# A hybrid decoder layer on one core: gate chunks beside the attention output projection, two plain blocks at the head of the second FFN, and the softmax combination's transfers on GpSimd's queue

## The chip, the cores and the metric

The kernel runs on one core of one Trainium2 chip. The metric is the time of one execution on the device, in microseconds (us), as the median of several runs. The engines are named as in the profile: PE is TensorE (the matmuls), PEld its weight loads, DVE is VectorE, ACT is ScalarE, POOL is GpSimd, SP is SyncE. SP computes nothing in this kernel and only issues DMAs; its issues are rows of "SPq".

## What is computed

One layer for 1024 prompt positions and 8 x 4 sample positions, 1056 rows of width 1024, in float32:

```
h  = LN1(alpha*x + 0.5*SwiGLU_a(x))                 # FFN-a, width 2816
z  = h @ w_in + b_in                                # q, k, v of 12 heads; u, v of the gMLP; gates gA, gB
A  = dilated sliding-window attention, 3 head groups (dilation 1, 4, 16), 4 heads each;
     head slot j of the 3 groups combined by their softmax denominators
B  = u * (tril(W_s) LN(v) + b)                      # gMLP, chunks of 128
h  = LN2(alpha*h + (sigmoid(gA)*(A@w_oa) + sigmoid(gB)*(B@w_ob)) @ w_out)
y  = LN3(alpha*h + 0.5*SwiGLU_b(h))                 # FFN-b
```

The updated key and value windows are outputs too; most of their bytes are copied from memory to memory (`ws<-st` in the profile).

## The kernel before, in words

**Layout.** Activations lie transposed, features on the 128 partitions and positions along the row. The 1056 positions are four chunks of 264 (`C`, `NC`). Every float32 operand is split into a high part (a cast on ACT, line 238) and a low part (a subtraction on DVE, line 239), and a product is three matmuls (`mm3`, line 227 for all of them). A product with a full 1024-row weight block is 24 matmuls for a chunk (`dense8`: a gate, a half of a plain FFN block, a block of w_out), one with w_ob 12, one with w_oa 6.

**Stages in order of time.** FFN-a (0 to about 650 us) and FFN-b (from about 1483) each have 22 blocks of 128 hidden features. Most blocks go through a Strassen-like scheme (`hidden`, seven products for all four chunks together, 168 matmuls); block 0 is computed plainly, chunk by chunk (`hidden8`, 48 matmuls a chunk), because a plain chunk can start as soon as its own layer norm is ready. In FFN-b the four chunks come out of LN2 one after the other. LN2 and LN3 are `norm`: column sums of squares on PE, a reciprocal root (`rsqrt`: a square root on ACT, line 630, and four small DVE operations), a broadcast by PE (line 597), scaling on DVE and ACT.

Between the FFNs comes `widen` (the input projection) and then `mix`, around which most of the change lies. In `mix` the PE's order is: ten "tail" gate blocks (6 block by block, then `LAST` = 4 together, chunk by chunk), then the w_ob products (`local(n)`, n = 0 to 5), then for each of the eight blocks n of w_oa: `product(wa, att, ...)` for the four chunks, each multiplied into the gate on DVE (line 1505), with `local(6)` and `local(7)` behind n = 0 and 1; then the sum of both branches (DVE, line 1583), its split, and w_out.

**What runs beside it.** Generators are advanced between these products (`tick`): `attend(i)` for six pairs of head slot and group (`bg`), the sample positions' attention (`slow`), the gMLP and the combination (`mid`). `attend` loads q, k and v of its pair from a scratch tensor (`fetch_qkv`, tiles `S<-zD`) and, at its start, those of the next pair; it ends with a transpose of the row maxima and sums (line 1225), which DVE copies out and a DMA writes to `mlD` (line 1229). After the third group of a head slot `combine(hp)` reads `mlD` back in another arrangement (lines 1247, 1249, 1253), computes the weights on DVE, writes them to `cD` (1276), reads them back spread over 64 partitions (1283) and scales and adds the three groups (1288 to 1291). The result, `att`, is split (`split_att`), and only then can w_oa start. All these transfers stand on SP's one queue, in order, between weights, gates and window copies.

**What sets the order.** Each engine executes its instructions in the order of the built program; a scheduler fixes it beforehand from priorities and a model of durations. Tiles come from pools of fixed size (37 large `S` slots, 8 weight buffers `W`, 2 raw buffers `R`, 3 + 5 PSUM banks `mm` and `ax`). An instruction that waits holds everything behind it on its engine.

Of the kernel before, what the change touches and what calls it, by code (L numbers as in the profile page):

```python
# [13 lines left out]
F32R = mybir.dt.float32r  # L14
AF = mybir.ActivationFunctionType
# [5 lines left out]
P = 128  # L21
# [43 lines left out]
WARM = 2  # L65
FENCED = (mybir.EngineType.DVE, mybir.EngineType.Activation, mybir.EngineType.SP)
# [4 lines left out]
LAST = 4  # L71
EARLY = 6
# [7 lines left out]
class Trunk:  # L80
# [131 lines left out]
    def unit(self, src, n=D, slot=False, ahead=URGENT):  # L212
        new = self.S if slot else self.W
        with self.tc.high_priority(offset=ahead):
            raw = self.R([P, D])
            hi, lo = new([P, D], F32R), new([P, D], F32R)
            dma = self.nc.sync.dma_start(raw[:, :n], src[:, :n])
            self.split(hi[:, :n], lo[:, :n], raw[:, :n])
        self.fence[mybir.EngineType.SP] = dma.ins
# [362 lines left out]
    def norm(self, c, i, mode, Y, s):  # L582
# [7 lines left out]
        r, t = self.X([P, 3], "rs"), self.X([P, 3], "rt")  # L590
        self.rsqrt(r, t, pv, EPL)
# [35 lines left out]

    def rsqrt(self, r, t, v, eps):
# [12 lines left out]
    def ffn(self, w13, w2p, w2, i, mode, resid):  # L641
        nc, preps = self.nc, {}
        last = FB + NG * (KB // 2) - 1
# [27 lines left out]
        else:  # L671
# [17 lines left out]
        def ready(f):  # L689
            for _ in preps.pop(f):  # L690
                pass
            if f < last:
                begin(f + 1)

        def between(f, bg, slow=0):
            if f + 1 in preps:
                next(preps[f + 1], None)
# [8 lines left out]
        for f in range(1, FB):  # L706
# [5 lines left out]
            def after():  # L712
# [4 lines left out]
            self.hidden(f, after)  # L717
# [400 lines left out]
    def attend(self, i):  # L1118
# [19 lines left out]
        self.fetch_qkv(i + 1)  # L1138
# [77 lines left out]
        for t in range(6):  # L1216
# [4 lines left out]
            if t < 4:  # L1221
                scores(t)
            yield from self.pause(SPREAD)
# [5 lines left out]
        nc.sync.dma_start(D_.rearrange("m h (i x) -> (m h i) x", x=P), mt)  # L1229
# [6 lines left out]
    def combine(self, hp):  # L1236
# [3 lines left out]
        for g in range(3):  # L1240
            x = raw[:, g]
            for m in range(2):
                for h in range(2):
                    src = self.mlD[hp, g, m, h]
                    o = x[8 * h : 8 * h + 8, m]
                    if g == 0:
                        nc.sync.dma_start(o, src.rearrange("(a x) -> a x", a=8))
                    elif g == 1:
                        nc.sync.dma_start(
                            o.rearrange("p (r b) -> p r b", r=4), src.rearrange("(r a b) -> a r b", r=4, a=8)  # L1250
                        )
                    else:
# [541 lines left out]
```

## Time and profile before

| | us |
|---|---|
| median of 3 runs | 2202.64 (2201.89 to 2203.19) |
| the profiled execution's own time | 2200.98 |
| its span, first to last instruction | 2199.2 |
| PE busy | 2133.2 |
| DVE busy | 1564.8 |
| ACT busy | 898.1 |
| POOL busy | 330.1 |

The profiled execution lies 1.66 us below the median. Of its own time, 1.8 us lie outside the span. PE is the engine with work nearly all the time, so time can be won where PE waits, or where it runs at a lower granted clock, and lost where PE gets more work or new waits. A window row of the profile gives busy time with the number of instructions in brackets for PE, PEld, DVE, ACT and POOL, then the granted PE clock, the busy share of the DMA engines and GB/s. A timeline row gives start, length, engine, line, operation, and in square brackets the idle time before it with what ended it.

### The profile page before, as it was taken

To read this page: it belongs to the slowest core of one execution; us is meant where nothing else is said; L and a number is where in the kernel's file an instruction comes from. 1 tells how busy PE (TensorE), PEld (TensorE's weight loads), DVE (VectorE), ACT (ScalarE), POOL (GpSimd) and SP (SyncE) were. 2 spreads that over 40 slices of the span, in tenths; PEclk is the share of its full clock that TensorE was granted. 3 is DMA by queue.
4 is the path that set the end of the run, shared out by engine and by line. 5 is a ranking of instruction groups with operands and counts; after the bars stand their busy time and mean duration, and the time that the engine had idled before them with its cause. 6 is when DMAs were issued, how large, how long until landed. Compare 5 with 4: busy or idle time off the path is not lost.

```text
span 2199.2 us, 43234 instructions
## 1 busy us (share of the span) xinstructions
PE 2133.2 (97%) x17281; PEld 2092.9 (95%) x17281; DVE 1564.8 (71%) x2718; ACT 898.1 (41%) x1690; POOL 330.1 (15%) x238
## 2 busy tenths in 40 slices
PE   9999999999998999999989998998999999999997
PEld 8999999999998999999879897998999999999997
DVE  8777776656788725887674648778676776657787
ACT  5444444421225634344465354246444444322224
POOL 0432332200010022232000000000432332100000
PEclk9999999999999999999989999999999999999999
DMA  4435545598873325666854547513445545596751
GB/s 157 146 134 177 179 161 177 193 367 324 330 279 136 135 102 188 215 215 221 313 165 152 172 156 245 187 51 126 165 158 178 171 161 185 186 384 264 295 192 79
DMA packets 170553, 429.82 MB, mean 195 GB/s; under 512 B 24864, under 2 KB 61456, under 8 KB 167664
## 3 DMA queue, kind: packets, MB, share of 16 engines
q1 hardware_dynamic: 169920, 426.53, 55.3%
q8 instruction: 135, 2.21, 0.4%
q10 hardware_dynamic: 432, 0.54, 0.1%
q14 instruction: 66, 0.54, 0.1%
HBM read 305.97 MB, written 167.22 MB: 215 GB/s over the span
## 4 chain that ended last, share of the span: by engine, by line
PE 81%; DMA 7%; DVE 7%; ACT 2%; issue 1%; POOL 1%; SPq 1%; ACTq 0%; DVEq 0%; POOLq 0%
PE ax L227 43%; PE mm L227 35%; DMA M<-kv 4%; DVE W L239 1%; PE ax L1164 1%; DMA zD<-M 1%; DMA S<-zD 1%; PE ax L1203 1%; DVE S L239 1%; PE ax L1187 1%; DMA R<-wz 0%; DVE X L1346 0%; DVE S L608 0%; DVE X L1361 0%; DVE M L1345 0%
## 5 line engine op out<-in xcount | busy, mean ns | idle before, releaser
L227 PE MATMUL ax<-S,W 128*128 128x264 f32 x5472 | 716.2, 284 | 0.8 <-ACT S L994 0.5
L227 PE MATMUL mm<-S,W 128*128 128x264 f32 x5040 | 677.4, 289 | 25.8 <-DVE S L1505 9.3
L227 PEld LDWEIGHTS ax<-S,W 128*128 128x128 f32 x5472 | 685.6, 188 | 3.3 <-ACT S L994 1.5
L227 PEld LDWEIGHTS mm<-S,W 128*128 128x128 f32 x5040 | 641.6, 191 | 43.1 <-issue 10.7
L227 PE MATMUL ax<-S,S 128*128 128x264 f32 x3288 | 483.7, 285 | 2.9 <-DVE S L1003 2.8
L227 PEld LDWEIGHTS ax<-S,S 128*128 128x128 f32 x3288 | 434.2, 188 | 4.1 <-DVE S L1003 4.1
L227 PE MATMUL mm<-S,S 128*128 128x264 f32 x2496 | 388.4, 286 | 9.0 <-ACT S L238 4.0
L227 PEld LDWEIGHTS mm<-S,S 128*128 128x128 f32 x2496 | 337.7, 189 | 11.5 <-ACT S L238 4.4
L238 ACT CAST W<-R 128x256 fp32r<-128x256 f32 (+2 forms) x172 | 127.6, 759 | 316.8 <-PE mm L227 118.2
L369 POOL TENSOR_TENSOR Q<-R 128x512 f32<-128x512 f32 x50 | 72.1, 1443 | 793.1 <-DMA R<-w13b 217.1
L239 DVE TENSOR_TENSOR W<-R,W 128x256 fp32r<-128x256 f32 (+2 forms) x172 | 152.6, 891 | 28.2 <-ACT W L238 24.0
L238 ACT CAST W<-Q 128x1024 fp32r<-128x1024 f32 (+1 forms) x79 | 77.9, 986 | 217.1 <-POOL Q L370 91.7
L780 DVE SCALAR_TENSOR_TENSOR S<-ax,S 128x264 f32<-128x264 f32 x240 | 99.9, 431 | 69.6 <-PE ax L227 68.5
L444 DVE TENSOR_TENSOR S<-ax,M 128x264 f32<-128x264 f32 x84 | 33.7, 433 | 150.6 <-PE ax L227 150.6
L106 POOL CAST S<-ones 128x1 fp32r<-128x1 f32 x32 | 18.3, 594 | 745.5 <-PE mm L227 663.8
L239 DVE TENSOR_TENSOR S<-Q,S 128x1024 fp32r<-128x1024 f32 (+1 forms) x79 | 111.8, 1415 | 3.5 <-ACT S L238 3.3
L239 DVE TENSOR_TENSOR W<-Q,W 128x1024 fp32r<-128x1024 f32 (+1 forms) x79 | 92.0, 1164 | 24.5 <-ACT W L238 24.5
L238 ACT CAST S<-Q 128x1024 fp32r<-128x1024 f32 (+1 forms) x79 | 77.8, 985 | 74.1 <-PE ax L227 55.0
L238 ACT CAST S<-R 128x512 fp32r<-128x512 f32 (+1 forms) x65 | 44.6, 686 | 116.5 <-DMA sumsA<-S 42.6
L239 DVE TENSOR_TENSOR S<-S,M 128x528 fp32r<-128x528 f32 x72 | 85.6, 1189 | 2.1 <-ACT M L238 0.2
L370 POOL TENSOR_TENSOR Q<-Q,R 128x512 f32<-128x512 f32 x50 | 83.6, 1673 | 2.7
L377 POOL TENSOR_TENSOR Q<-R,Q 128x512 f32<-128x512 f32 x50 | 82.7, 1653 | 1.2
(199 smaller groups left out, 2063.3 us busy)
## 6 DMA issues: line engine op xcount, KB each, us to landing
ws<-st SPq DMA_DIRECT2D x144, 256.0 KB
S<-sumsA SPq DMA_DIRECT2D x63, 528.0 KB
S<-sumsB SPq DMA_DIRECT2D x63, 528.0 KB
M<-kv SPq DMA_DIRECT2D x96, 256.0 KB
sumsA<-M SPq DMA_DIRECT2D x90, 264.0 KB
sumsB<-M SPq DMA_DIRECT2D x90, 264.0 KB
R<-w13b SPq DMA_DIRECT2D x44, 512.0 KB
S<-zD SPq DMA_DIRECT2D x42, 528.0 KB
```

What stands on the lines that cost most here:

```text
L106: self.nc.gpsimd.tensor_copy(t[:, 0, :1] if len(shape) == 3 else t[:, :1], self.ones[:, :1])
L227: mm = lambda a, b, s, e: nc.tensor.matmul(o, a[:, cc], b, start=s, stop=e, skip_group_check=True)
L238: a = self.nc.scalar.copy(hi, src)
L239: b = self.nc.vector.tensor_tensor(lo, src, hi.bitcast(F32), op=ALU.subtract)
L369: tt(s12[:, lo], cd[:, lo], cd[:, hi], op=ALU.add)
L370: tt(s12[:, hi], s12[:, lo], ab[:, lo], op=ALU.subtract)
L377: tt(s34[:, hi], ab[:, hi], s12[:, hi], op=ALU.subtract)
L444: go(one, 5, False, lambda x: tt(h[:, x, 1], one[x], p7[:, x], op=ALU.add))
L780: nc.vector.scalar_tensor_tensor(y(x, r, e), bank[x], HALF, y(x, r, e), op0=ALU.mult, op1=ALU.add)
L1164: nc.tensor.matmul(pS[h][:, r, :nk], q[e, i * P : (i + 1) * P], k[e, k0 : k0 + nk], start=True, stop=True)
L1187: nc.tensor.transpose(pT[r][:, h, o], s[:, r, h, o], self.ident)
L1203: nc.tensor.matmul(pv[0][e, (i % 4) * P : (i % 4 + 1) * P], V[:, i - (nb - 1) + b, e], sT[:, r, h, b * P : b * P + P], start=b == 0, stop= ...
```

## The change

It has seven parts.

1. **Gates.** `LAST` goes from 4 to 3. The last three gate blocks are computed for chunks 0 to 2 where they were; their chunk 3 is computed by `beside` behind w_oa blocks 2, 4 and 5 (`BESIDE`), and ACT writes it straight into the gate's tile. All eight `local(n)` now stand ahead of w_oa, and three gate tiles are fetched ahead instead of two.
2. **Plain head of FFN-b.** Blocks 0 and 19 (before: block 0) are computed plainly there, chunk by chunk.
3. **Reciprocal root on DVE.** `rsqrt_dve` (a start value by integer arithmetic and three Newton steps, 11 DVE operations) takes the place of `rsqrt` in chunk 3 of LN2, in chunk 2 of LN3 and in the gMLP's norm. After chunk 2 of LN2 a one-column Silu stands on ACT.
4. **Combination on GpSimd's queue.** The writes to `mlD` and `cD` and the reads of both are issued by POOL. Group 0's four reads become one. The third group's weights are read once the loop has begun.
5. **q, k, v.** The next pair's are fetched at the fourth step of `attend`, not at its start.
6. **gMLP.** Two pauses instead of one between the norm's transposes; the sample rows' scale and shift move into a generator of their own, `sgu_rows`, at the end.
7. **`narrow`.** The w_oa and w_ob weights keep high and low part in one `W` buffer.

The order that the scheduler makes of it, at three places. First, the DMA issues of the combination. Before, on SP, for head slot 0 (a row gives line, operation, what is written and what is read, and the shape; `zD`, `bD`, `mlD` and `cD` are scratch tensors in memory, `R<-wo` a weight, `ws<-st` a window copy):

```order
L1229 DMA mlD<-X_14123 32x128
L1102 DMA S_14164<-zD_8646 128x1056
L1247 DMA S_14177<-mlD 8x128 x4
L1249 DMA S_14177<-mlD 8x4x32 x4
L1253 DMA S_14177<-mlD 8x16x8 x4
L955 DMA zD_8660<-M_14306 128x264
L955 DMA zD_8660<-M_14402 128x264
L955 DMA zD_8660<-M_14470 128x264
```

Now, on POOL, for head slot 1, from the second last pair's maxima to the end of the combination:

```order
L1267 DMA mlD<-X_14920 32x128
L1282 DMA S_15276<-mlD 16x2x128
L1287 DMA S_15276<-mlD 8x4x32 x4
L1267 DMA mlD<-X_15235 32x128
L1287 DMA S_15276<-mlD 8x16x8 x4
L1311 DMA cD<-S_15276 16x128 x3
L1321 DMA S_15306<-cD 64x1024 x2
L1321 DMA S_15309<-cD 64x1024 x2
L1321 DMA S_15344<-cD 64x1024 x2
```

The transfers have left SP's order, and the last head slot's groups 0 and 1 are read ahead of the last pair's write (`X_15235`). Behind that write stand 4 + 3 + 6 issues of the combination, all on POOL.

Second, PE in the w_oa stage. Before, the last product of w_oa block 0 (weights `W_15864` and `W_15865`) is followed by w_ob's block 6:

```order
L227 MATMUL mm_15964<-S_15857,W_15864 128x264
L227 MATMUL mm_15964<-S_15858,W_15864 128x264
L227 MATMUL mm_15964<-S_15857,W_15865 128x264
L227 MATMUL mm_15997<-S_13534,W_15990 128x264
L227 MATMUL mm_15997<-S_13535,W_15990 128x264
L227 MATMUL mm_15997<-S_13534,W_15991 128x264
```

Now the last product of w_oa block 2 (one buffer, `W_15995`) is followed by chunk 3 of a gate (`W_14740` and `W_14741`, 24 matmuls):

```order
L240 MATMUL mm_16030<-S_15893,W_15995 128x264
L240 MATMUL mm_16030<-S_15894,W_15995 128x264
L240 MATMUL mm_16043<-S_12735,W_14740 128x264
L240 MATMUL mm_16043<-S_12736,W_14740 128x264
L240 MATMUL mm_16043<-S_12735,W_14741 128x264
```

The gate's 72 matmuls have moved from the attention into this stage, and the 96 of `local(6)` and `local(7)` out of it. Between the last transpose of the row maxima and the first w_oa matmul PE had 198 matmuls with w_ob; now it has 252.

Third, ACT at the head of FFN-b. Before (line 415 is the Silu of a plain block, 630 the square root of the norm, `L328` a cast of the Strassen sums):

```order
L415 ACT_TABLE_LOAD
L415 ACTIVATE M_17638<-mm_17588 128x264
L238 CAST S_17150<-S_16387 128x1056
L328 CAST S_17488<-S_17456 128x1056
L328 CAST S_17522<-S_17411 128x1056
L328 CAST S_17554<-S_17490 128x1056
L630 ACT_TABLE_LOAD
L630 ACTIVATE X_17571<-ax_17567,eps_165 128x3
L415 ACT_TABLE_LOAD
L415 ACTIVATE M_17714<-mm_17664 128x264
```

Now (610 is the one-column Silu, 428 the Silu of a plain block):

```order
L659 ACTIVATE X_17366<-ax_17362,eps_165 128x3
L610 ACT_TABLE_LOAD
L610 ACTIVATE X_17372<-X_17366 128x1
L251 CAST S_17314<-R_17313 128x1024
L589 ACTIVATE M_17490<-S_16362 128x264
L251 CAST W_17557<-R_17556 128x1024
L635 ACTIVATE S_16352<-S_16352,cols 128x264 x4
L251 CAST W_17564<-R_17563 128x1024
```

One table load is left, ahead of the weights of block 19 (the two casts to `W`). On PE the broadcast of chunk 3's norm is followed by 24 matmuls and the wait for that chunk before; now 130 matmuls of other chunks and blocks lie between.

The diff, cut to its core:

```diff
-LAST = 4
-EARLY = 6
+LAST = 3
+BESIDE = {2: 13, 4: 14, 5: 15}
...
+    def narrow(self, src, n):
+        with self.tc.high_priority(offset=URGENT):
+            raw = self.R([P, D])
+            both = self.W([P, D], F32R)
+            hi, lo = both[:, :n], both[:, n : 2 * n]
+            dma = self.nc.sync.dma_start(raw[:, :n], src)
+            self.split(hi, lo, raw[:, :n])
...
+        if c == NC - 1 and i == 1 or c == NC - 2 and mode == "out":
+            self.rsqrt_dve(r, t, self.X([P, 3], "rx", 1), pv, EPL)
+        else:
+            self.rsqrt(r, t, pv, EPL)
+        if i == 1 and c == NC - 2:
+            nc.scalar.activation(self.X([P, 2], "warm", 1)[:, :1], r[:, :1], AF.Silu)
...
+    def rsqrt_dve(self, r, t, x, v, eps):
+        nc.vector.tensor_scalar(x, v, eps, None, op0=ALU.add)
+        nc.vector.tensor_scalar(r.bitcast(I32), x.bitcast(I32), -0.5, MAGIC, op0=ALU.mult, op1=ALU.add)
+        for _ in range(3):
+            nc.vector.tensor_tensor(t, x, r, op=ALU.mult)
+            tt(t, t, -0.5, r, op0=ALU.mult, op1=ALU.mult)
+            self.chain = tt(r, t, 1.5, r, op0=ALU.add, op1=ALU.mult).ins
...
+        plain = PLAIN[: 1 if i == 0 else 2]
...
+            lead = [units] + [[self.unit(w13[f, x]) for x in range(2)] for f in plain[1:]]
             begin(1)
             for c in range(NC):
                 self.drain(lns.pop(c))
-                self.hidden8(units, 0, c)
-                if c:
-                    with self.chained():
-                        next(preps[1], None)
-            self.bg.append(s1)
+                if c == NC - 1:
+                    self.bg.append(s1)
+                    self.step(self.bg, 2)
+                for f, u in zip(plain, lead):
+                    self.hidden8(u, f, c)
...
-        self.fetch_qkv(i + 1)
+        follower = i + 1
...
+            if t == 3:
+                self.fetch_qkv(follower)
...
-        nc.sync.dma_start(D_.rearrange("m h (i x) -> (m h i) x", x=P), mt)
+        nc.gpsimd.dma_start(D_.rearrange("m h (i x) -> (m h i) x", x=P), mt)
...
+            if g == 0:
+                nc.gpsimd.dma_start(x, src.rearrange("m h (a x) -> (h a) m x", a=8))
+            else:
+                r = GROUPS[g][1]
+                for m in range(2):
+                    for h in range(2):
+                        nc.gpsimd.dma_start(
+                            x[8 * h : 8 * h + 8, m].rearrange("p (r b) -> p r b", r=r),
+                            src[m, h].rearrange("(r a b) -> a r b", r=r, a=8),
+                        )
...
-            nc.sync.dma_start(self.cD[hp, g].rearrange("h (a x) -> (h a) x", a=8), t[g][:, 1])
+            nc.gpsimd.dma_start(self.cD[hp, g].rearrange("h (a x) -> (h a) x", a=8), t[g][:, 1])
...
+                    nc.gpsimd.dma_start(cbs[-1][64 * h : 64 * h + 64], self.cD[hp, g, h].partition_broadcast(64))
...
-            yield
+            yield from self.pause(2)
...
-        self.rsqrt(rs[:, 0], rs[:, 1], mv[:, :, 1], EPS)
+        self.rsqrt_dve(rs[:, 0], rs[:, 1], mv[:, :, 1], mv[:, :, 1], EPS)
...
+        def fetch_gate(n):
+            held = 26 + n in [DENSE[m] for m in units]
+            t = self.S([P, NT])
+            cc = slice(0, (NC - 1) * C if held else NT)
+            nc.sync.dma_start(t[:, cc], self.zD[26 + n][:, cc])
+            return t
+
+        def beside(n):
+            m = DENSE[n] - 26
+            p = self.mm_tile()[:, :C]
+            self.dense8(p, units.pop(n), NC - 1)
+            with self.urgent():
+                nc.scalar.activation(ta[m][:, -C:], p, AF.Identity, bias=self.bin(DENSE[n]))
...
-        for n in range(EARLY):
+        for n in range(KB):
             local(n)
...
+            if n in BESIDE:
+                beside(BESIDE[n])
```

More of the change, by code (lines that the diff above doesn't have):

```diff
@@ L642, in ffn @@
         nc, preps = self.nc, {}
-        last = FB + NG * (KB // 2) - 1
+        plain = PLAIN[: 1 if i == 0 else 2]
+        blocks = [f for f in range(FB) if f not in plain] + [FB + g for g in range(NG * (KB // 2))]
+        after = dict(zip(blocks, blocks[1:]))
         def begin(f):
@@ L704, in load @@
                     loads.popleft()()
-        for f in range(1, FB):
+        for f in blocks[: FB - len(plain)]:
             ready(f)
```

91 lines of the change are left out of this document (48 added, 43 removed).

## The prediction

> **What bounds the kernel now.** I read the totals first, then busy time by window, then who waited for whom, then the timelines of the places that stood out.
>
> ```profile
> span 2199.2 us, 43234 instructions
> PE 2133.2 (97%) x17281; PEld 2092.9 (95%) x17281; DVE 1564.8 (71%) x2718; ACT 898.1 (41%) x1690; POOL 330.1 (15%) x238
> 100.00:150.00 50.00, 50.00 (x413) 50.00 (x412) 36.16 (x47) 20.32 (x37) 17.29 (x11) 1.00 0.43 148
> ```
>
> PE is busy in 2133.2 of 2199.2 us, so waits cost it 66 us. Where nothing disturbs it (third row, within FFN-a) it does 413 matmuls in 50 us, 8.26 a us. I use that rate as a ruler: matmuls missing from a window are time lost there, by waits and by a lower clock together. Four windows from 1333 us on, the w_oa stage, and four from 1490 us on, the head of FFN-b, fall far short:
>
> ```profile
> 1333.00:1343.00 10.00, 4.59 (x23) 4.38 (x24) 8.55 (x14) 5.74 (x7) 0.00 (x0) 0.81 1.03 363
> 1343.00:1353.00 10.00, 9.75 (x70) 9.44 (x70) 7.96 (x14) 2.98 (x4) 0.00 (x0) 0.85 0.58 199
> 1353.00:1363.00 10.00, 8.60 (x68) 8.13 (x66) 9.69 (x17) 3.98 (x6) 0.00 (x0) 1.00 0.63 211
> 1363.00:1373.00 10.00, 7.74 (x56) 6.81 (x54) 9.77 (x19) 6.50 (x8) 0.00 (x0) 1.00 0.79 272
> 1373.00:1383.00 10.00, 7.21 (x42) 6.47 (x42) 9.47 (x14) 3.67 (x5) 0.84 (x1) 0.83 0.53 176
> 1490.00:1500.00 10.00, 8.13 (x68) 7.92 (x67) 8.42 (x10) 9.92 (x13) 0.00 (x0) 1.00 0.19 73
> 1500.00:1510.00 10.00, 7.51 (x60) 7.09 (x59) 8.85 (x15) 5.20 (x9) 0.00 (x0) 0.99 0.31 83
> 1510.00:1520.00 10.00, 8.08 (x47) 7.77 (x48) 9.58 (x13) 4.99 (x6) 0.00 (x0) 0.66 0.60 220
> 1520.00:1530.00 10.00, 9.52 (x79) 9.31 (x78) 7.73 (x10) 5.65 (x9) 0.00 (x0) 1.00 0.15 57
> ```
>
> The first five rows hold 23 + 70 + 68 + 56 + 42 = 259 matmuls, worth 31.4 us: 18.6 us of 50 are lost. The last four hold 254, worth 30.8 us: 9.2 us of 40 are lost. The clock column shows the second part of such a loss: 0.66 to 0.85 in the slices after a long wait. From 1353 on DVE is busy 9.5 us or more in ten. There the stage is bound by DVE, not by PE.
>
> **The change part by part.** *The head of FFN-b.*
>
> ```profile
> 1493.94 2.83 PE L227 MATMUL mm<-S,S 128*128 128x264 f32 x21 [1.87 <-ACT M L415]
> 1504.74 3.15 PE L227 MATMUL ax<-S,W 128*128 128x264 f32 x24
> 1511.91 0.81 PE L227 MATMUL mm<-S,S 128*128 128x264 f32 x2 [4.02 <-ACT S L238]
> 1497.79 1.28 ACT L630 ACT_TABLE_LOAD   x1
> 1499.37 1.28 ACT L415 ACT_TABLE_LOAD   x1
> ```
>
> The 4.02 us are PE waiting for chunk 3 of LN2, with only 24 matmuls as cover since the broadcast. The new order has 130 matmuls at that point, 130 / 8.26 = 15.7 us, against 3.15 + 4.02 us needed. So this wait goes, with its slow clock. The 1.87 us are a full set of PSUM banks while ACT loads the Silu table; the one-column Silu brings that load forward, and the two loads of the last two rows go because the root is on DVE. The price is arithmetic: block 19 takes 4 x 48 = 192 matmuls instead of 168, and 24 / 8.26 = 2.9 us. What hides its weights is block 0 on PE (5.8 us a chunk); without that cover a load like `R<-w13b` is late next. I leave 1.0 us of the 9.2 lost, for the first Strassen sums. Term: -9.2 + 1.0 + 2.9 = **-5.3 us**, bounded by -6.3 (nothing left) and +2.9 (the whole loss reappears there).
>
> *The end of the attention: cover.*
>
> ```profile
> 1309.29 0.27 PE L1225 MATMUL ax<-ident,X 128*32 128x128 f32 x1
> 1336.15 4.19 PE L227 MATMUL mm<-S,W 128*128 128x264 f32 x21 [3.18 <-DVE S L1505]
> 1342.60 1.01 PE L227 MATMUL mm<-S,W 128*128 128x264 f32 x3 [2.26 <-ACT S L238]
> 1309.90 0.32 SPq L1229 DMA_DIRECT2D mlD<-X  x1
> 1313.02 1.40 SPq L1253 DMA_DIRECT2D S<-mlD  x4
> 1322.60 1.26 SPq L1276 DMA_DIRECT2D cD<-S  x3
> 1324.02 3.04 SPq L1283 DMA_DIRECT2D S<-cD  x5
> 1328.20 0.46 SPq L1283 DMA_DIRECT2D S<-cD  x1
> 1315.95 0.40 DVE L1263 TENSOR_TENSOR X<-X,S 16x128 f32<-16x128 f32 x1
> 1329.24 1.23 DVE L1288 TENSOR_TENSOR S<-S,S 128x1024 f32<-128x1024 f32 x1 [1.61 <-DMA S<-cD]
> 1337.81 1.22 DVE L1290 TENSOR_TENSOR S<-S,S 128x1024 f32<-128x1024 f32 x1
> 1342.57 1.23 DVE L239 TENSOR_TENSOR S<-S,S 128x1024 fp32r<-128x1024 f32 x1 [1.01 <-ACT S L238]
> ```
>
> From the last maxima (1309.29) to the last split of `att` (1342.57 + 1.23 = 1343.8) the combination takes 34.5 us. PE has 198 w_ob matmuls to put over it, 24.0 us, and then waits. With the change it has 252, 30.5 us, and some 0.7 us of small ones, 31.2 us. The 72 gate matmuls do not cover this; they stand behind the first w_oa blocks.
>
> *The same chain on POOL's queue.* No row shows a DMA issued by POOL, so call its price p us an issue. From the rows above: 0.6 to the write; 3.1 - 0.3 + p until it has landed; 4p for the third group's reads and 1.5 (2.93 from issue to use, less 1.40 of issues); 6.65 for the weights on DVE; 3p for `cD` and 1.1 until the first lands; 6p for the spread reads and 4.1 for the last to land (1329.24 less the first two issues' 1.1 from 1324.02); 5.0 for one group's product, sum and split. Sum: C = 21.8 + 14p. On SP's queue p was 0.3 to 0.5, but the last read stood behind two 528 KB loads and arrived only at 1337.81, 9.6 us after its issue at 1328.20; a queue of its own doesn't stand behind those. The bounds of p are SP's 0.32 and the longest plain POOL group:
>
> ```profile
> L106 POOL CAST S<-ones 128x1 fp32r<-128x1 f32 x32 | 18.3, 594 | 745.5 <-PE mm L227 663.8
> L377 POOL TENSOR_TENSOR Q<-R,Q 128x512 f32<-128x512 f32 x50 | 82.7, 1653 | 1.2
> ```
>
> POOL's smallest operation takes 0.594 us, its long ones 1.653. I take p = 1.0, nearer to the small one, since an issue handles few bytes. Then C = 35.8 us, and 35.8 - 31.2 = 4.6 us stay uncovered.
>
> The rows give DVE as 65 to 98% busy in this stretch. On the page "SBUF — State Buffer" (section "SBUF: two separate sides", with the figures in the section after it) the Trainium skill states that DMAs issued by GpSimd have descriptors written by software, which stops while DVE runs certain operations on both ports, and gives 620 ns alone against 3100 ns beside a DVE copy. No row here shows either. By 0.62 C would be 30.5 us, by 3.1 it would be 65.2, an estimate from that page alone.
>
> *The w_oa stage behind it.*
>
> ```profile
> 1375.90 1.25 DVE L1583 TENSOR_TENSOR S<-S,S 128x1056 f32<-128x1056 f32 x1
> 1377.06 1.10 DVE L1505 TENSOR_TENSOR S<-S,mm 128x264 f32<-128x264 f32 x3
> 1378.70 1.26 DVE L239 TENSOR_TENSOR S<-S,S 128x1056 fp32r<-128x1056 f32 x1 [0.53 <-ACT S L238]
> ```
>
> A block n costs DVE 1.10 + 0.43 for four chunk products, 1.25 for the sum, 1.26 for the split and some 0.4 for a weight: 4.5 us, eight blocks 36 us, with two w_out splits of 1.2 about 38. PE has 192 w_oa and 72 gate matmuls, 264 / 8.26 = 32.0 us. The gates need no DVE, and `local(6)` and `local(7)`, which did, are gone from here. So 6 us stay lost instead of what DVE costs now. Lost after: 4.6 + 6.0 = 10.6 against 18.6. Term: **-8.0 us**; at p = 0.32 nothing is uncovered and it is -12.6, at p = 1.65 it is 13.7 + 6.0 - 18.6 = +1.1.
>
> *The attention before it.*
>
> ```profile
> PE ax L1187 <- ACT S L1176: 10.0, 4, 5.9
> PE mm L227 <- ACT M L954: 5.0, 3, 2.9
> PE ax L1144 <- DMA S<-zD: 1.3, 1, 1.3
> ```
>
> The waits here come to some 18 us. The root on DVE removes two table loads (1.28 each by the rows above) near the 5.9 us wait, and the pauses thin out what ACT does there. Against that q, k and v arrive later: only 1.3 us is now waited for such a load (third row). Up to five pairs can newly wait, and what is queued behind the waiting transpose is all of PE. I take no net gain: **0**, between -8 (the first two rows halved) and +8 (1.3 + some for each of five pairs).
>
> *Small parts.* Chunk 2 of LN3 takes 7 more DVE operations of 0.16 us while PE still multiplies: **+0.5**, between 0 and 1.1. `narrow` saves buffers and no instruction, and `sgu_rows` moves work that nobody waits for: 0; if the weights came late, one load.
>
> **Sum.** -5.3 - 8.0 + 0 + 0.5 = -12.8 us. The profiled execution took 2201.0, so 2188.2; the median lies 1.7 us above it, so **2189.8 us**.
>
> **The rivals.** *POOL's issues are dear (slower).* If each issue also waits for the DVE instruction then running (1.25 us for those rows), p = 2.25, C = 53.3, and 22.1 + 6.0 us are lost: +9.5 in place of -8.0, and 2207 us. The whole change turns from gain to loss at p = 1.9, or at C = 48.6 us. For it: DVE is full from 1353 on and 14 issues stand in one chain. Against it: POOL does nothing else there (0.00 busy). The Trainium skill's lock, cited above, is this mechanism; by its 3.1 us the time would be 2219, an estimate from the page.
>
> *The waits move into the attention (no change).* The fetches at the fourth step leave each pair only two or three gate chunks of lead, and each of five V transposes waits 2 us for 1.6 MB: +10 there, 2200 us. For it: the 1.3 us row and a load of 9 us at 1328. Against it: 1.6 MB less stand in front of the first pair's loads.
>
> *Everything works (faster still).* p near SP's 0.32 and half the attention's ACT waits gone: -5.3 - 12.6 - 6.0 + 0.5, 2179 us.
>
> **How the numbers follow.** The forecast's own cases (2182 to 2197) get 0.5, everything works 0.13, the attention rival 0.17, dear issues 0.20. Eight in ten lie between 2178 and 2210: the lower end is the last rival's, the upper that of the slower one with some attention waits. About 0.2% (4.4 us) is what a measurement can tell from no change. Faster by more (below 2198.2): 0.5 + 0.13 + 0.05 of the attention rival = 0.68; within: 0.12; slower: 0.20.
>
> **What would show it.** Right: the 4.02 and 1.87 us waits at the head of FFN-b gone, block 19 with 192 `mm` matmuls; PE's wait ahead of the first w_oa product about 5 us instead of 5.4 with slow matmuls between; DVE still full behind it; POOL's DMA rows near 1 us. Wrong: those rows at 2 us or more, the last `S<-cD` landing later than 45 us after the last maxima, or new waits of PE for `S<-zD`.

## The result, and the profile after

| | median, us | executions |
|---|---|---|
| before | 2203.38 (2200.07 to 2208.03) | 14 |
| changed | 2204.27 (2200.14 to 2209.72) | 14 |

The ratio is 1.0001, 95% interval 0.9992 to 1.0010: no difference that can be measured, where 2189.8 was forecast. The profiled execution of the changed kernel took 2209.72 us, the slowest of the 14; a second profile of it (`e13_again`, own time 2202.89) lies near the median and is used beside it. The totals of the first:

```profile
span 2207.8 us, 43311 instructions
PE 2137.7 (97%) x17305; PEld 2098.3 (95%) x17305; DVE 1556.8 (71%) x2731; ACT 889.3 (40%) x1678; POOL 343.9 (16%) x276
```

PE has 24 matmuls and 4.5 us of busy time more, and the idle time around it is 4 us longer. Two groups of windows, the last maxima to the first w_oa blocks and the head of FFN-b (columns as in the prediction):

```profile
1304.00:1314.00 10.00, 9.54 (x82) 9.08 (x81) 6.58 (x23) 3.03 (x6) 2.94 (x5) 1.00 0.37 110
1314.00:1324.00 10.00, 6.38 (x42) 6.17 (x41) 6.32 (x19) 0.53 (x1) 1.51 (x3) 0.85 0.78 268
1324.00:1334.00 10.00, 6.35 (x45) 6.14 (x44) 2.69 (x4) 5.15 (x7) 3.09 (x6) 0.84 0.80 202
1334.00:1344.00 10.00, 4.25 (x18) 3.66 (x17) 4.92 (x5) 3.77 (x4) 0.00 (x0) 0.50 0.60 161
...
1505.00:1515.00 10.00, 10.00 (x85) 10.00 (x84) 9.78 (x16) 6.82 (x9) 0.00 (x0) 1.00 0.51 182
1515.00:1525.00 10.00, 10.00 (x85) 10.00 (x84) 9.70 (x19) 4.39 (x7) 0.00 (x0) 1.00 0.32 94
1525.00:1535.00 10.00, 10.00 (x85) 10.00 (x83) 7.17 (x11) 3.56 (x5) 0.00 (x0) 1.00 0.61 227
```

In these three windows FFN-b's head is full: 85 matmuls in 10 us, no wait, clock 1.00. Just ahead of them one new wait stands, for the low part of a weight:

```profile
1504.29 4.61 PE L240 MATMUL mm<-S,W 128*128 128x264 f32 x36 [1.56 <-DVE W L252]
```

The loss has moved: from 1314 to 1344 PE does 42 + 45 + 18 = 105 matmuls, worth 12.7 us, in 30 us. DVE is not full there (2.7 of 10 us in one window), and the clock falls to 0.50. PE, DVE and POOL in these 50 us (timeline rows: start, length, engine, line; in brackets the wait and what ended it):

```profile
1305.36 9.04 PE L240 MATMUL mm<-S,W 128*128 128x264 f32 x72
1314.27 3.18 PE L240 MATMUL mm<-S,W 128*128 128x264 f32 x24
1321.06 7.55 PE L240 MATMUL mm<-S,W 128*128 128x264 f32 x48 [3.62 <-DVE S L1551]
1332.27 3.01 PE L240 MATMUL mm<-S,W 128*128 128x264 f32 x12 [3.65 <-DVE S L1551]
1338.71 2.98 PE L240 MATMUL mm<-S,W 128*128 128x264 f32 x12 [3.43 <-DVE S L1551]
1344.64 5.63 PE L240 MATMUL mm<-S,W 128*128 128x264 f32 x31 [2.95 <-DVE S L1551]
```

```profile
1304.55 1.09 DVE L1551 TENSOR_TENSOR S<-S,mm 128x264 f32<-128x264 f32 x3
1330.65 1.23 DVE L1330 TENSOR_TENSOR S<-S,S 128x1024 f32<-128x1024 f32 x1 [5.15 <-DMA S<-cD]
1331.79 0.42 DVE L1551 TENSOR_TENSOR S<-S,mm 128x264 f32<-128x264 f32 x1
1337.00 1.23 DVE L1332 TENSOR_TENSOR S<-S,S 128x1024 f32<-128x1024 f32 x1 [4.79 <-DMA S<-cD]
1338.14 0.42 DVE L1551 TENSOR_TENSOR S<-S,mm 128x264 f32<-128x264 f32 x1
1340.64 1.23 DVE L1332 TENSOR_TENSOR S<-S,S 128x1024 f32<-128x1024 f32 x1 [2.08 <-DMA S<-cD]
1351.26 1.22 DVE L252 TENSOR_TENSOR S<-S,S 128x1024 fp32r<-128x1024 f32 x1
```

```profile
1305.20 0.53 POOL L1267 DMA_DIRECT2D mlD<-X  x1 [18.63 <-DVE S L1551]
1308.89 1.95 POOL L1287 DMA_DIRECT2D S<-mlD  x3 [3.16 <-DMA mlD<-X]
1311.15 0.59 POOL L1287 DMA_DIRECT2D S<-mlD  x1 [0.32 <-issue]
1319.04 1.52 POOL L1311 DMA_DIRECT2D cD<-S  x3 [7.30 <-DVE S L1309]
1324.85 3.19 POOL L1321 DMA_DIRECT2D S<-cD  x6 [4.28 <-PE mm L240]
```

POOL's issues are cheap, 0.5 to 0.6 us each in these rows. But DVE stands three times (12.0 us) for the spread read of `cD`. The `mm` multiplications (line 1551), which empty PE's banks, stand behind those waits in DVE's order, and PE stops three times (10.0 us) until one has run. The 3.62 us ahead of them are taken up under "The wait that was left". The landing times of the last write and reads of `cD` (min/median/max):

```profile
L1311 POOL DMA_DIRECT2D cD<-S x3: 487/511/523, 1319.0 to 1320.1; - x3
DMA to landing us min/median/max: 4.9/5.2/5.3
...
L1321 POOL DMA_DIRECT2D S<-cD x6: 509/518/526, 1324.8 to 1327.5; - x6
DMA to landing us min/median/max: 3.8/9.7/13.0
```

For all runs, "lost" is a stage's length less its large matmuls at 0.121 us (1 / 8.26) and its small ones at their usual spacing: what waits and a slow clock cost. Attention is from the first transpose of V to the last maxima, the stretch from there to the first w_oa product (before 198, now 252 w_ob matmuls), then the w_oa stage.

| run | median, us | ratio to before (95%) | profiled execution | lost: attention | stretch | w_oa |
|---|---|---|---|---|---|---|
| before | 2203.4 | 1 | 2201.0 | 41.5 | 5.2 | 15.5 |
| changed | 2204.3 | 1.0001 (0.9992, 1.0010) | 2209.7 | 46.1 | 21.4 | 7.5 |
| e13_again | 2204.2 | 0.9999 (0.9985, 1.0013) | 2202.9 | 41.4 | 18.4 | 7.3 |
| e1_sp_queue | 2205.1 | 0.9998 (0.9988, 1.0008) | 2197.5 | 44.0 | 14.5 | 5.6 |
| e2_gates_pool | 2197.9 | 0.9974 (0.9962, 0.9985) | 2200.1 | 38.0 | 17.4 | 6.4 |
| e3_no_beside | 2201.6 | 0.9983 (0.9974, 0.9992) | 2201.7 | 40.4 | 14.0 | 11.4 |
| e4_head_only | 2199.6 | 0.9982 (0.9972, 0.9993) | 2198.9 | 47.0 | 4.3 | 17.7 |
| e5_later | 2194.5 | 0.9965 (0.9951, 0.9978) | 2194.7 | 40.6 | 11.9 | 7.2 |
| e6_pool_later | 2194.2 | 0.9962 (0.9949, 0.9975) | 2194.2 | 40.0 | 13.6 | 7.4 |
| e7_sp_later | 2201.6 | 0.9992 (0.9983, 1.0002) | 2201.3 | 44.2 | 13.9 | 7.3 |
| e8_pool_only | 2216.2 | 1.0063 (1.0050, 1.0076) | 2216.5 | 47.0 | 19.1 | 11.7 |
| e9_gates_first | 2193.9 | 0.9947 (0.9928, 0.9965) | 2195.2 | 44.8 | 9.6 | 9.2 |
| e10_early_qkv | 2198.0 | 0.9967 (0.9952, 0.9982) | 2210.6 | 43.1 | 22.7 | 6.7 |
| e11_no_beside_later | 2197.3 | 0.9970 (0.9956, 0.9984) | 2196.1 | 40.0 | 7.1 | 12.8 |
| e12_best | 2192.0 | 0.9941 (0.9923, 0.9960) | 2190.9 | 37.3 | 8.9 | 10.2 |
| e14_late_qkv_only | 2198.8 | 0.9973 (0.9960, 0.9986) | 2200.8 | 38.9 | 3.0 | 19.7 |
| e15_gates_only | 2205.1 | 1.0003 (0.9990, 1.0016) | 2203.0 | 44.2 | 15.6 | 6.2 |
| e16_spread | 2191.8 | 0.9954 (0.9939, 0.9968) | 2192.6 | 35.9 | 1.2 | 17.8 |

Medians are compared by the ratio, since the kernel before drifted between 2202.7 and 2204.7 from one set of runs to the next. The lost columns are of one execution each. Even the first 690 us, where nothing differs, vary by 4 us between profiles. The attention column is the coarsest: its level depends on the spacing taken for the small matmuls, and another choice for it lowers the whole column by 10 to 14 us. One of the 12 executions of `e14_late_qkv_only` took 3437.8 us at a granted clock of 0.56 and is not in its ratio.

### The profile page after: what moved, and what is told of

Read it like the earlier page. It is cut to its first block, busy times and chain, and to the rows that moved or that the text cites. A ratio compares the mean times of both kernels' runs of the same rounds, so it can differ in the third digit from the quotient of the medians.

```text
span 2207.8 us, 43311 instructions
## 1 busy us (share of the span) xinstructions
PE 2137.7 (97%) x17305; PEld 2098.3 (95%) x17305; DVE 1556.8 (71%) x2731; ACT 889.3 (40%) x1678; POOL 343.9 (16%) x276
## 4 chain that ended last, share of the span: by engine, by line
PE 84%; DMA 7%; DVE 5%; ACT 2%; issue 1%; POOL 1%; SPq 0%; ACTq 0%; DVEq 0%; POOLq 0%
PE ax L240 45%; PE mm L240 36%; DMA M<-kv 3%; DMA S<-zD 1%; DVE W L252 1%; DMA R<-wz 1%; PE ax L1200 1%; DVE S L252 1%; DMA S<-cD 1%; PE ax L1239 0%; PE ax L1223 0%; DVE S L627 0%; DMA zD<-M 0%; ACT S L1212 0%; DVE X L1403 0%
## 5 line engine op out<-in xcount | busy, mean ns | idle before, releaser
L240 PE MATMUL mm<-S,W 128*128 128x264 f32 x5208 | 700.5, 290 | 32.2 <-DVE S L1551 16.7
L240 PEld LDWEIGHTS mm<-S,W 128*128 128x128 f32 x5208 | 666.3, 192 | 47.2 <-DVE S L1551 15.6
L240 PE MATMUL ax<-S,W 128*128 128x264 f32 x5400 | 706.9, 284 | 0.9 <-ACT S L1030 0.7
L240 PEld LDWEIGHTS ax<-S,W 128*128 128x128 f32 x5400 | 676.3, 188 | 3.9 <-ACT S L1030 1.9
L240 PE MATMUL ax<-S,S 128*128 128x264 f32 x3240 | 476.6, 284 | 2.7 <-DVE S L1039 2.7
L240 PEld LDWEIGHTS ax<-S,S 128*128 128x128 f32 x3240 | 427.7, 188 | 3.8 <-DVE S L1039 3.8
L240 PE MATMUL mm<-S,S 128*128 128x264 f32 x2472 | 383.6, 285 | 2.6 <-DVE S L252 2.3
L251 ACT CAST W<-R 128x1024 fp32r<-128x1024 f32 (+3 forms) x173 | 128.9, 761 | 342.4 <-PE mm L240 150.4
L252 DVE TENSOR_TENSOR W<-R,W 128x1024 fp32r<-128x1024 f32 (+3 forms) x173 | 151.1, 877 | 29.5 <-ACT W L251 29.2
```

The lines of the kernel that those rows point to most:

```text
L240: mm = lambda a, b, s, e: nc.tensor.matmul(o, a[:, cc], b, start=s, stop=e, skip_group_check=True)
L251: a = self.nc.scalar.copy(hi, src)
L252: b = self.nc.vector.tensor_tensor(lo, src, hi.bitcast(F32), op=ALU.subtract)
```

## The experiments

**Which queue, and what meets the reads.**

`e1_sp_queue`, all five kinds of transfer back on SP:

```diff
-            nc.gpsimd.dma_start(self.cD[hp, g].rearrange("h (a x) -> (h a) x", a=8), t[g][:, 1])
+            nc.sync.dma_start(self.cD[hp, g].rearrange("h (a x) -> (h a) x", a=8), t[g][:, 1])
```

> The changed kernel with the combination's transfers (the write and read of mlD, the write and read of cD) back on SP's queue; all else as changed. The changed kernel's median is 2204.3 us. Theory A (shared engines): on a queue of its own the spread read of cD no longer stands behind SP's loads, but it shares the 16 DMA engines with the three 528 KB gate loads that SP issues at the same moment, so the last read lands 13 us after its issue and DVE, which waits for it in order, keeps PE's banks full. On SP's queue most of the read stands ahead of those gates again: about 6 us faster, 2198. Theory B (held buffers): the three gate blocks whose chunk 3 is put off hold six of the eight weight buffers and four large slots through the combination, and w_ob's weights, gates and the spread read wait for buffers whatever queue issues them: 2204, within 3. Theory C (POOL's issues are dear) is out by the rows of 0.52 us an issue; it would give a gain of 10 or more.

2205.1: no gain, against theory A as stated. The profile, its fastest execution, shows the same stop with the reads on SP:

```profile
1320.08 1.22 DVE L1330 TENSOR_TENSOR S<-S,S 128x1024 f32<-128x1024 f32 x1 [7.06 <-DMA S<-cD]
```

```profile
1322.99 7.24 PE L240 MATMUL mm<-S,W 128*128 128x264 f32 x38 [8.60 <-DVE S L1551]
```

So the stop is not tied to POOL's queue. Theory B's 2204 fits the time; the next runs test its mechanism.

`e2_gates_pool`:

```diff
-            nc.sync.dma_start(t[:, cc], self.zD[26 + n][:, cc])
+            (nc.gpsimd if n < 3 else nc.sync).dma_start(t[:, cc], self.zD[26 + n][:, cc])
```

> The changed kernel, with one edit: the first three gate loads of the w_oa stage are issued by POOL, behind the six spread reads of cD, and not by SP beside them. The order on PE and ACT is the same to the instruction. Theory A (shared engines): the reads, 1.57 MB, have the engines almost to themselves and land within some 8 us instead of 13; DVE's three waits for cD, 12.0 us in sum, fall to 6 or less, PE's three waits of 3 to 3.7 us behind them shrink with them: 5 us faster, 2199. The gates land about 7 us after the last read, when the first w_oa products are done, so 1 or 2 us of the gain may go there. Theory B (held buffers): the spread read is issued as late as before and the weights come as late: 2204, within 2.

2197.9, as theory A has it. Three loads issued behind the reads, not beside them, gain 6 us; PE and ACT keep their order, and on DVE two splits stand elsewhere. By the trace's DMA records, the KB per us that each queue moved:

```
changed        1326 to 1340   POOL 112   SP 142   (1573 KB of cD in 14 us)
e2_gates_pool  1322.5 to 1336 POOL 235   SP  29   (the 1573 KB of cD, then the gates)
e8_pool_only   1336 to 1350   POOL 112   SP 154
before         1324 to 1340   -          SP 272
```

With loads on both queues each moves about half of the bytes, so the read takes 14 us. Nearly alone, POOL's queue moves 235 KB a us: the queue itself is not slow. DVE's waits for `cD` fell from 12.0 to 5.9 us. Against the second profile of the changed kernel the difference is smaller: the packets of the read took 10.5 us there and 9.3 here, and DVE waited 7.9 us for them. So the traces show the sharing, but only about 2 us of the 6 when an execution near the median is taken.

`e8_pool_only`, the kernel before with part 4 of the change alone, the combination on POOL's queue:

> The kernel before, with the combination's transfers on POOL's queue and nothing else of the change. Theory A: the write of cD lands 5.0 us after its issue where it was read 1.4 us after it on SP, and the spread read shares the engines with SP's loads; DVE's waits for cD (2.4 us in sum before) grow by about 6 us and most of it reaches PE: 2208, between 2205 and 2212. If the queue as such costs nothing and only the changed order around it does (held buffers, cover, DVE's order): 2203, within 2.

2216.2, 13.3 us slower than before in the same set, more than either theory had. Its DVE and PE, where before they waited 1.61 and 3.18 us:

```profile
1342.91 1.23 DVE L1292 TENSOR_TENSOR S<-S,S 128x1024 f32<-128x1024 f32 x1 [8.48 <-DMA S<-cD]
```

```profile
1348.78 4.53 PE L227 MATMUL mm<-S,W 128*128 128x264 f32 x21 [11.56 <-DVE S L1509]
```

```profile
L1273 POOL DMA_DIRECT2D cD<-S x3: 487/511/523, 1332.8 to 1333.9; - x3
DMA to landing us min/median/max: 1.6/1.6/1.6
L1283 POOL DMA_DIRECT2D S<-cD x6: 509/517/526, 1335.0 to 1337.7; - x6
DMA to landing us min/median/max: 4.7/9.7/13.5
```

The write landed in 1.6 us here and in 5.2 in the changed kernel, where four 528 KB gate loads were in flight: which fits a small write that, on a queue of its own, still comes behind the bytes that the engines have taken on (`e5_later` and `e16_spread`, with and without such loads at that moment, had 5.6 and 1.6). No run varies those loads alone. The reads met SP's loads and took up to 13.5 us.

**Held buffers.** `e3_no_beside`, chunk 3 of the last gates where it was:

```diff
-            if c < NC - 1:
-                for n in units:
-                    self.gate8(units[n], DENSE[n], c, AF.Identity, STEPS["tail"], 1)
+            for n in units:
+                self.gate8(units[n], DENSE[n], c, AF.Identity, STEPS["tail"], 1)
+        units = self.A = None
```

> The changed kernel, but chunk 3 of the last three gate blocks is computed where it was, with the other chunks, and nothing is put off behind w_oa; so no gate block holds weight buffers or slots through the combination. The combination stays on POOL's queue. Theory B (held buffers): ACT's waits for a weight buffer (5.2 and 8.4 us), POOL's wait of 4.3 us for a slot and the 3.6 us wait of PE go, the combination ends some 8 us earlier and the stage behind it, with 72 matmuls less and bound by DVE at about 38 us, stays as long as it is: the 72 matmuls now stand in the attention as before (8.7 us), so 2204 + 8.7 - 1.5 (shorter w_oa stage) - 10 = about 2201. Theory A: the reads meet the gate loads as before, nothing is gained in the combination and the 8.7 us come on top, less 1.5: 2211.

2201.6 is theory B's number, and by the ratios 0.2% below the changed kernel, but of B's mechanism little showed. POOL waited 4.0 us ahead of the reads here too, and in `e16_spread`, with the gate blocks held, it waited 0.9 us where the write had landed in 1.6: that wait is the landing of the write, not a slot. ACT's waits for a weight buffer behind PE did not shrink (26.1 us, against 15.4). What changed is SP's order: its three gate loads went out at 1319.21, ahead of the reads (1326.77), which landed in 4.8 to 7.4 us. The last split came 40.3 us after the last maxima, against 48.4 and 45.4 in the two profiles of the changed kernel.

**DVE's order.** `e5_later` makes the three multiplications wait for a later w_ob multiplication:

```diff
+        while hp and len(self.muls) <= 24:
+            yield
...
-            if g == 0:
-                nc.vector.tensor_tensor(att[:, :NP], aT, cb, op=ALU.mult)
-            else:
-                nc.vector.tensor_tensor(aT, aT, cb, op=ALU.mult)
+            with self.tc.issue_after(self.muls[24]) if hp else ExitStack():
+                nc.vector.tensor_tensor(att[:, :NP] if g == 0 else aT, aT, cb, op=ALU.mult)
```

> The changed kernel, with DVE's three multiplications of the last combination by the spread weights (the ones that wait for the read of cD) put behind 17 of the w_ob chunk products that follow the last maxima, where 12 stood ahead of them. Queues, loads and work as changed. Theory D (DVE's order): PE's cover is only what stands ahead of the waiting multiplication in DVE's order and three PSUM banks more, since each w_ob product is multiplied out of its bank by DVE. Five more products are 60 matmuls, 7.3 us of the 10.0 us that PE waits in three pieces: 2204.3 - 6 = 2198. Theory A alone (shared engines): the last read lands as late as before, the products moved ahead only leave less to do behind it: no gain, 2204, within 2.

2194.5, 9.7 us faster than the changed kernel by the medians and 7.9 by the ratios, through an order alone. The reads still took up to 11.3 us to land; PE had work meanwhile:

```profile
1318.24 15.59 PE L240 MATMUL mm<-S,W 128*128 128x264 f32 x108 [4.73 <-DVE S L1553]
1334.26 3.17 PE L240 MATMUL mm<-S,W 128*128 128x264 f32 x24 [0.43 <-ACT W L251]
```

```profile
L1321 POOL DMA_DIRECT2D S<-cD x6: 509/518/526, 1321.5 to 1324.1; - x6
DMA to landing us min/median/max: 7.0/8.8/11.3
```

The edit moved more than the three multiplications. PE's and POOL's orders are as in the changed kernel, but ACT's and SP's shifted, and SP's three gate loads went out at 1313.64, ahead of the reads, where they went at 1325.91, beside them. The reads came no earlier for that: the last one landed 36.8 us after the last maxima, against 36.5. So the gain comes from what DVE does before it waits, not from quicker reads.

`e6_pool_later` adds the edit of `e2_gates_pool`; `e7_sp_later` adds the later multiplications to `e1_sp_queue`.

> Both edits: the first three gate loads on POOL's queue behind the spread reads (alone: 2197.9, -6.4), and the three multiplications behind 17 products. Theories A and D side by side: the edit of the gates left waits of PE of 4.4, 1.1, 2.1 and 2.5 us in this stretch, the last three behind DVE's waits for cD; they go, and with them the slow clock that follows: 2197.9 - 6 = 2192. If both edits take away the same waits (the gate edit had already taken those that the order costs), 2197.

> The combination on SP's queue (alone: 2205.1, no gain) with the three multiplications behind 17 products. Theory D: there DVE waited 7.1 and 1.9 us for cD and PE 8.6 us behind it; most of that goes: 2198. Theory A would have had the gain already from SP's queue alone, which did not come; under A with D against it, 2205.

2194.2 and 2201.6, where 2192 or 2197 and 2198 were expected. The two edits take the same waits away and do not add. On SP's queue less is won: DVE stood 9.7 us there for a gate load, `S<-zD`, that SP issues between the reads.

**The wait that was left.** `e9_gates_first` (on top of `e5_later`):

```diff
-            wb = self.narrow(a["wo"][n, :, 2 * P :], 4 * P)
+            with self.tc.issue_after(gate[-1]) if n >= 6 else ExitStack():
+                wb = self.narrow(a["wo"][n, :, 2 * P :], 4 * P)
```

> The kernel with the later multiplications (2194.5), and on SP's queue the four gate loads of the last w_ob blocks put ahead of the last two w_ob weights, where they stood behind them. What is left there is a wait of PE of 4.7 us, of which DVE stands 1.9 us for such a gate load. Theory B in its narrow form: the held gate blocks leave two of eight weight buffers, so a w_ob weight waits on SP for a buffer, and the gate loads behind it come late. With the gate loads ahead that wait goes: 2194.5 - 4 = 2190.5. If the loads wait for slots of their own (freed by the end of the attention), they come no earlier, and the weights, now behind them, come late: 2195 to 2198.

2193.9, no difference from `e5_later` beyond its interval, and the wait stayed at 4.40 us. `e11_no_beside_later` combines `e3_no_beside` and `e5_later`:

> No gate block put off (alone: 2201.6) and the three multiplications behind 17 products. Theory D: its DVE waits of 9.7 us for cD, and the 2.8 and 5.8 us of PE behind them, mostly go: 2201.6 - 6 = 2195.6. With no held buffers no gate load of w_ob is late here, so the 4.7 us wait that the later multiplications alone left should not appear: PE's waits between the last maxima and the first w_oa product under 4 us in sum. If held buffers cost nothing, the wait is there as well and the time is 2198 to 2200.

2197.3, and a wait of 2.81 us at the same place without any held block. So neither late gate loads nor held buffers make it. `e16_spread` (on top of `e12_best`, below) spreads the weights' small DVE operations between the multiplications:

```diff
+K1, K2, K3 = 16, 17, 18
...
+        behind = lambda k: self.tc.issue_after(self.muls[k]) if hp else ExitStack()
+        with behind(K1):
+            nc.vector.tensor_tensor(raw[:, :, 1], raw[:, :, 1], raw[:, :, 0], op=ALU.mult)
...
...
+        with behind(K2):
...
+            nc.vector.reciprocal(mn, mn)
+        with behind(K3):
```

> The fastest so far (2192.0) with the nine small operations of the last combination's weights spread between the w_ob multiplications in DVE's order, where they stood in one block; the work is the same. Left in its stretch was one wait of PE of 4.4 us, which neither the moved gate loads nor giving up the held gate blocks removed. If that wait is again DVE's order (5 us of weights in which no PSUM bank is emptied, against three banks of 1.45 us each): it falls under 1 us, and the time to 2188 or 2189. If PE waits there for loads: the wait stays, and the write of cD comes up to 4 us later, 2192 to 2195.

```profile
1297.00 9.03 PE L241 MATMUL mm<-S,W 128*128 128x264 f32 x72
1305.88 0.27 PE L1443 MATMUL ax<-ident,X 128*128 128x128 f32 x1
1305.90 23.30 PE L241 MATMUL mm<-S,W 128*128 128x264 f32 x189
1339.57 1.03 PE L241 MATMUL mm<-S,W 128*128 128x264 f32 x3 [10.37 <-ACT S L252]
```

The wait is gone, as expected of DVE's order: 72 + 189 matmuls run without a stop. The time is not better: 2191.8. PE now reaches the end of its cover and waits 10.4 us in one piece for the split of `att`. Only here does the forecast's picture hold, cover against chain: 32 us of work against 45 us from the last maxima (1295.68) to the last split of `att` (1340.8). Even this chain has a stop of another kind in it. On DVE, between the second and the third multiplication, stands the split of a weight:

```profile
1334.06 0.39 ACT L252 CAST W<-R 128x256 fp32r<-128x256 f32 x1
1334.48 0.43 DVE L253 TENSOR_TENSOR W<-R,W 128x256 fp32r<-128x256 f32 x1 [4.82 <-ACT W L252]
```

ACT makes the high part of that weight only behind three gates, for whose loads it waited 6.8 us. The third multiplication ran at 1335.96, though its read had landed by 1331.7. No run moves this split.

**The other parts alone.** `e4_head_only`, `e14_late_qkv_only` and `e15_gates_only` are the kernel before with one part each; `e10_early_qkv` is the changed kernel with the fetches early; `e12_best` is `e9_gates_first` with the fetches early; `e13_again` is the changed kernel.

```diff
+        self.fetch_qkv(i + 1)
...
-            if t == 3:
-                self.fetch_qkv(follower)
```

> The kernel before with the head of FFN-b alone: blocks 0 and 19 plain, the root on DVE in chunk 3 of LN2 and chunk 2 of LN3, the one-column Silu. Gates, combination, attention and gMLP as before. The forecast's term for it was -5.3 us and +0.5 at the end: 2203.4 - 4.8 = 2198.6. If the terms stand side by side, it shows 2198 to 2200, and the changed kernel loses as much in the combination. If the head's gain is only what the lost time moves to (a clock that runs slower after, a wait further on), it shows 2203.

> The changed kernel with q, k and v of the next pair fetched at the start of attend again, as before; all else as changed. PE waits 4.9 us in three pieces for these loads in the changed kernel's profile, 1.3 us in one before. If the later fetch costs time by itself: 3 to 4 us faster, 2200 to 2201. If it only moves the loads away from the combination's transfers, which then collide again: 2204 or slower, up to 2208. The forecast took it for nothing, between -8 and +8 for all edits of the attention.

> The kernel before with q, k and v fetched at the fourth step of attend and nothing else of the change. If the late fetch costs by itself what its undoing gave (6 us): 2209. If it costs only beside the combination on POOL's queue: 2204, within 2. The forecast had it at nothing.

> The kernel before with the gates' part alone: three gate blocks' chunk 3 put off behind w_oa, all w_ob blocks ahead, one weight buffer for high and low part. Combination on SP's queue and the attention as before. The forecast's term for this was -8 together with the queue. If the cover works as forecast where the transfers are not on POOL's queue: -8 to -12, 2192 to 2196. If held buffers and DVE's order eat it there too: 2200 to 2205. The sum of the parts measured alone (head -4.7, queue +13.3, late fetch up to +6) leaves -14 for it and the small rest.

> The fastest so far (later multiplications, gate loads of w_ob ahead of the last two weights: 2193.9) with q, k and v of the next pair fetched early again. If the early fetch is worth the same here as in the changed kernel (6 us there): 2188. If part of that was the same wait in the combination that the two other edits take away: 2191 to 2194.

> The changed kernel once more, not edited, for a second profile: the first one is of the slowest of its 14 executions, 5.4 us above the median. Between the last maxima and the first w_oa product that profile lost 21.4 us. If the loss there is the same in any execution: 20 to 22. If it depends on how the loads meet: 14 to 18 in an execution near the median of 2204.

The head alone gives 0.18%, 4.0 us of the mean ratio and 4.7 by the medians: the forecast's term. The gates' part alone gives nothing: its stretch loses 15.6 us, with 10.9 us of it in one wait of PE behind DVE. The late fetch alone gains 5.8 us, where 2204 or 2209 was expected, and undoing it in the changed kernel gains 6.3 as well. So it has no price of its own; that it depends on what else is in flight is a guess, and no profile shows where the 6 us are. The one of `e10_early_qkv` is of its slowest execution, 12.6 us above its median. `e12_best`, at 2192.0, is 0.6% faster than before (0.9941, 0.9923 to 0.9960) and faster than the changed kernel. The second profile of the changed kernel loses 18.4 us in the stretch, so some 3 of the first one's 21.4 belong to that slow execution.

## Why the prediction was wrong, point by point

- **The head of FFN-b: right.** Forecast -5.3 and +0.5 at the end; alone 4.7 faster. Both waits are gone. Where 1.0 us was to stay lost, one new wait of 1.56 us came.
- **The w_oa stage: right in size.** 6.0 us were to stay lost; 7.5 and 7.3 did, against 15.5 before. The stage took 39.3 us, where DVE's work was put at about 38. (The first windows of the prediction's table, called four, are the five that its sum counts.)
- **The cover: a step that failed.** "With the change it has 252, 30.5 us" counted every w_ob matmul behind the last maxima as cover. A w_ob product, 12 matmuls, needs DVE to empty its bank. From the last maxima (1304.03) to the first multiplication that waits for `cD`, DVE empties 12 banks; the first three (1304.55) were filled earlier, since PE's next w_ob matmul comes at 1305.36. So 9 of the 21 products stand ahead of the wait, three more fit into the banks, and PE has 12 x 12 = 144 matmuls, 17.4 us. Its rows stop there for the first of the three waits: 72 + 24 + 48 (the stop in between is that of "The wait that was left"). The same count gives the stop in other profiles: 144 in `e13_again` and `e2_gates_pool`, 132 in `e3_no_beside` (8 ahead), 96 in `e1_sp_queue` and `e15_gates_only` (5 ahead). `e5_later` puts 14 ahead and `e16_spread` more, and PE's stops go.
- **What that step cost.** The stretch and the w_oa stage were to lose 4.6 + 6.0 = 10.6 us. They lost 28.9 and 25.7 in the two profiles of the changed kernel, and 19.1 and 19.0 in `e5_later` and `e16_spread`. So DVE's order is worth some 7 to 10 us. About 8 us more than forecast stay lost when it is mended, and they are the chain's.
- **The chain: the other step that failed, 35.8 us in the forecast and 48.4 in the profile.** The second profile has 45.4, `e5_later` 44.9 and `e16_spread` 45.1, so it stays long when PE's stops are gone. By the forecast's own sum 48.4 would leave 17.2 us uncovered even with all 252 matmuls as cover: +4.6 in place of -8.0, no change in all.
- **Where the chain's time went: p too dear, the rest too cheap.** p was 0.53, not 1.0, so 21.8 + 14p is 29.2 us. The profile has 1352.48 - 1304.03 = 48.4. By hops, formula in brackets: 15.0 to the first write of `cD` (14.2); 5.8 to the first read's issue (2.7), where the write lands in 5.2 us; 15.8 to the last read's use (7.3); 11.8 to the last split (5.0), with other DVE work in between. The second and third came from "a queue of its own doesn't stand behind those". It does not stand behind SP's loads, but it shares the engines with them. The Trainium skill says so, in "DMA: Bandwidth & Descriptors", section "Issuing engines are not separate DMA queues": transfers started by SP, ACT or GpSimd run on the same 16 engines and interleave. The 112 beside 142 KB a us agree, and 235 nearly alone.
- **What SP's queue had cost was read too high.** The prediction's "arrived only at 1337.81" takes the multiplication's start for the landing. That row shows no wait, and by the trace's DMA records the last packets of that read ended at 1336.0, 7.8 us after the issue, not 9.6.
- **The attention: 0 was right in sum** (41.5 before, 41.4 in the second profile). But that is luck as far as the runs tell: it hides the fetches' 6 us of either sign, which stay unexplained.
- **The rivals.** Dear issues named the right place and the wrong mechanism: the landings were dear, not the issues. Of the signs set for it, rows of 2 us or more did not come, and the last read landed 36.5 us after the last maxima, not 45. The Trainium skill's lock ("SBUF — State Buffer", section "SBUF: two separate sides") does not show in these rows: no issue took over 0.68 us, beside whatever DVE did. Nor does it explain the write's 5 us in the changed kernel by itself: DVE stood idle for 2.42 of them (1321.69 to 1324.11). The attention rival's 2200 us and no change come closest to the result, but by luck: waits for `S<-zD` in the attention grew from 1.3 to 4.9 us, less than its 10, and the loss came in the stretch behind. A time within 4.4 us of no change had been given 0.12.
- **The parts are not independent.** Head -4.7, queue +13.3, late fetch -5.8 and gates +0.5 make +3.3 for parts measured alone; the whole is 0.0 (0.9999, 0.9985 to 1.0013). That sum proves nothing, since the four intervals together leave it open by about 5 us. Single parts do: the queue costs 13.3 us in the kernel before, and taking it back in the changed kernel (`e1_sp_queue`) gains nothing. The gMLP's part was not tried alone.

## What to carry to other kernels

Work covers a wait only if the engine that has to drain it does not itself stand in that wait: count the products ahead of the waiting instruction in the draining engine's order, without those that lay in the banks at the start, add the free banks, and no more. Before moving a transfer to another queue, list what is in flight on all queues when it starts; a queue takes it out of an issue order, not off the shared engines. When a stop is removed, work out the chain's own length first: it is what remains when the cover is used up.

## What the runs showed of the hardware that was not expected

- A write of 24 KB in three DMAs on GpSimd's queue landed in 1.6 to 1.8 us when little else was in flight (`e8_pool_only`, `e16_spread`) and in 4.9 to 6.4 us when SP's 528 KB loads were (the changed kernel, `e5_later`, `e9_gates_first`). The issue took 0.5 us in both cases.
- With loads in flight on two queues, one moved 112 and the other 142 KB a us (changed kernel); nearly alone, GpSimd's moved 235 (`e2_gates_pool`).
- Two kernels that run the same instructions on PE and ACT in the same order (`e2_gates_pool` and the changed one) differ by 6 us through three loads on another queue (and two splits that stand elsewhere on DVE).
